# Weight units 64 bytes on in the ring of a hybrid retention and neighbourhood-attention block, with three products split in two

## The chip, the cores and the metric

The kernel runs on one core of one Trainium2 chip. The metric is the device time of one launch in microseconds (us). One matmul instruction of TensorE (PE) multiplies a stationary operand of 128 x 128, the weights of the array, which a separate instruction loads (PEld), by a moving operand of 128 rows and up to 512 columns that is read from on-chip memory (SBUF), and adds the product up in an accumulator bank. VectorE (DVE), ScalarE (ACT) and GpSimd (POOL) do the elementwise work, SyncE (SP) issues most of the transfers.

## The reference

Two layers over 256 latent and 256 context tokens of width 1024. Layer 0 mixes by retention with 4 heads (for both kinds of tokens), layer 1 by neighbourhood attention with 32 heads (latent tokens only, with keys and values from all 512). A squared-relu MLP of 4096 hidden units follows each. Shifts, scales and gates come from a conditioning vector.

```python
for i in range(DEPTH):                      # 2 layers
    mod = silu(c) @ ada_w[i] + ada_b[i]     # shifts, scales, gates; the same for the context
    h = x * (1.0 + sc1) + sh1
    hc = ctx * (1.0 + sc1c) + sh1c
    y, yc = mixer(h, hc)                    # retention in layer 0, neighbourhood attention in layer 1
    x = layer_norm(DN_ALPHA * x + g1 * y, ln_g[i, 0], ln_b[i, 0])
    h = x * (1.0 + sc2) + sh2
    x = layer_norm(DN_ALPHA * x + g2 * sq_relu_mlp(h, mlp_w1[i], mlp_w2[i]), ln_g[i, 1], ln_b[i, 1])
    # layer 0 does the same for ctx
```

## The kernel before

**Products.** All large products are made from float32 numbers split in a high and a low part, both in the fast 32-bit matmul type (fp32r). A product is three passes into one accumulator, high by high, high by low, low by high (`mm3`, line 174). In the program's names `hTh` and `hTl` are the high and low parts of the activations, transposed, 8 blocks of 512 token columns; `hi` and `lo` are those of the weights. The three passes of one block therefore read in the trace `hTh,hi`, `hTl,hi`, `hTh,lo`: first the moving operand, then the weights.

**Stages and moving widths.** Layer 0's projections move 512 columns (`pq`, `pv`, `pg`, `pw`). Its MLP moves 512 columns too, but for the first two of eight pairs of hidden blocks in the first half: there the latent tokens go first (256 columns, `mm1(..., LAT, ...)`), then the context tokens (256 columns, `ctx_mm1`, line 1278), because the context's layer norm is not done yet. In layer 1 the queries and the first pair of key blocks move 256 columns (`pn`; `q_mm`, line 1461, and `k_mm`), the other keys and the values 512 (`pn`, `pnv`). Layer 1's MLP moves 256 columns with an offset: its activations are stored from column `AT = 7 * LINE` on (line 1949), 448 bytes into each block; `p1t` is its first part.

**The weights' ring.** Weights arrive in units of 512 KB, 128 partitions by 1024 numbers (four blocks of 256 columns or two of 512). SP's queue transfers a unit into one of four raw tiles; ACT casts it to the high part; DVE subtracts to get the low part (`fetch`, line 258; `lows`, line 284). High parts go round in a pool `hip` of five tiles and low parts in a pool `lop` of five (lines 139 and 140), and `take` (line 289) has units prepared up to five ahead of their use. The eight chunks of the first stage use the same pools (`Weights.high` and `.low`, lines 763 and 768).

**Where things stand.** Small constants (`lnT`, `cT`, `scol`, `bcol`, `acol`, `misc`, `lgn`, four `mod` tiles) stand in one pool, `cpool`, ahead of `hTh` and of everything large; pools follow each other without gaps. Sizes before, in bytes for each partition: 16384 for each of `hTh` and `hTl`, 4096 for each raw, high or low tile. All of these are multiples of 128, so from a block of `hTh` or `hTl` to any weight block the distance is a multiple of 128 bytes, but in layer 1's MLP, where 448 bytes make it an odd multiple of 64. `LINE` is 16 numbers, 64 bytes. In the built program `hTh` starts at byte 40608 of a partition, which is 32 past a multiple of 64.

**The order of work.** Each engine runs its instructions in order. In the first MLP's early part and in the whole of layer 1's mixer PE, ACT and DVE are held to the program's order (`InOrder` with `on` set). Elsewhere a scheduler puts instructions in the order of their readiness by its own estimate; SP is always held to the program's order.

Of the kernel before, what the change touches and what calls it, by code (L numbers as in the profile page):

```python
# [10 lines left out]
F32 = mybir.dt.float32  # L11
F32R = mybir.dt.float32r
# [5 lines left out]
P = 128  # L18
D = 1024
KC = D // P  # L20
# [4 lines left out]
DK = 256  # L25
DV = 512
# [10 lines left out]
LINE = 16  # L37
# [67 lines left out]
def kernel(  # L105
# [23 lines left out]
    pe, act, dve, pool, sp = (  # L129
        InOrder(tc, getattr(nc, e), e in PIN)  # L130
        for e in ("tensor", "scalar", "vector", "gpsimd", "sync")
    )
    ec = ctx.enter_context

    WB = 5
    smp = ec(tc.tile_pool(name="smp", bufs=4))
    cpool = ec(tc.tile_pool(name="cpool", bufs=1))
    rawp = ec(tc.tile_pool(name="rawp", bufs=4))
    hip = ec(tc.tile_pool(name="hip", bufs=WB))
    lop = ec(tc.tile_pool(name="lop", bufs=WB))  # L140
# [11 lines left out]
    def nm(s):  # L152
        uid[0] += 1
        return f"{s}_{uid[0]}"
# [4 lines left out]
    def slot(i, shape, dt, s):  # L159

        return arena.tile(shape, dt, tag=f"s{i}", name=nm(s))

    def scr(s, dt=F32):
        return scp.tile([P, 512], dt, tag="scr", name=nm(s))

# [5 lines left out]
        act.copy(out=hi_ap, in_=raw_ap)  # L171
        (eng or dve).tensor_sub(out=lo_ap, in0=raw_ap, in1=hi_ap.bitcast(F32))

    def mm3(o, a, b, start, stop):
        (ah, al), (bh, bl) = a, b
        pe.matmul(o, lhsT=ah, rhs=bh, start=start, stop=False)
        pe.matmul(o, lhsT=ah, rhs=bl, start=False, stop=False)
        pe.matmul(o, lhsT=al, rhs=bh, start=False, stop=stop)


# [1 line left out]

    specs = []

    def w_rows(wt, r0, nr, c0, ncol):
        specs.append((wt[r0 : r0 + nr, c0 : c0 + ncol], nr // P, ncol))

    WI, WO = ret_w_in[0], ret_w_o[0]
# [12 lines left out]
            for u in range(2):  # L201
                w_rows(WO, h * DV + u * 256, 256, half * 512, 512)

    def spec_w1(l, f0):
        for u in range(2):
            w_rows(mlp_w1[l], 512 * u, 512, f0, 256)

    for hf in range(2):
        for fp in range(8):
            spec_w1(0, hf * 2048 + fp * 256)  # L210
        for half in range(2):
            for u in range(8):
                w_rows(mlp_w2[0], hf * 2048 + u * 256, 256, half * 512, 512)

    NW, NWO = nat_w_in[0], nat_w_o[0]

    def spec_nq(base, gp):
        for u in range(2):
            w_rows(NW, 512 * u, 512, base + gp * 256, 256)

    def spec_nv(half):
        for u in range(4):
# [31 lines left out]
    units = []  # L254
# [3 lines left out]
    def fetch(n, in_scratch=False, at=None):  # L258

        for src, k, ncol in specs[len(units) : len(units) + max(n, 0)]:  # L260
            raw = rawp.tile([P, k, ncol], F32, tag="raw", name=nm("raw"))
            sp.dma_start(out=raw[:], in_=src.rearrange("(k p) n -> p k n", p=P))
            if len(units) in scaled_units:
                dve.tensor_mul(
                    out=raw[:], in0=raw[:], in1=scale_row[0].unsqueeze(1).broadcast_to([P, k, ncol])
                )
            if in_scratch or len(units) in scratch_units:
                hi, lo = Rows([scr("hi", F32R) for _ in range(k)]), Rows([scr("lo", F32R) for _ in range(k)])
                for i in range(k):
                    act.copy(out=hi[:, i, :], in_=raw[:, i, :])  # L270
                    pending.append((lo[:, i, :], raw[:, i, :], hi[:, i, :]))
                units.append((hi, lo))
                continue
            if at is None:
                hi = hip.tile([P, k, ncol], F32R, tag="hi", name=nm("hi"))
                lo = lop.tile([P, k, ncol], F32R, tag="lo", name=nm("lo"))
            else:
                both = slot(at, [P, 2, k, ncol], F32R, "hilo")
                hi, lo = both[:, 0], both[:, 1]
            act.copy(out=hi[:], in_=raw[:])  # L280
            pending.append((lo[:], raw[:], hi[:]))
            units.append((hi, lo))
# [32 lines left out]

    ident = cv("ident")

    lnT = cpool.tile([P, 2, 2, 2, KC], F32, tag="lnT", name="lnT")
    cT = cpool.tile([P, KC, 16, 2], F32, tag="cT", name="cT")
    scol = cpool.tile([P, 2, KC], F32, tag="scol", name="scol")  # L320
    bcol = cpool.tile([P, 2, KC], F32, tag="bcol", name="bcol")
    acol = cpool.tile([P, 3, 2, KC], F32, tag="acol", name="acol")
    COLUMNS = (0, 1), (1, 0), (1, 1)
    lns = dram.tile([64, P], F32, tag="lns", name="lns")

# [40 lines left out]
    still = scr("still", F32R)  # L366
    dve.memset(still[:, :256].bitcast(F32), 1.0)

    misc = cpool.tile([P, 40], F32, tag="misc", name="misc")
    mhalf, onecol, lgm = misc[:, 0:1], misc[:, 1:34], misc[:, 36:40]  # L370
    dve.memset(mhalf[:], -0.5)

    lgn = cpool.tile([P, 2, 8], F32, tag="lgn", name="lgn")
    mods = {}
    for l in range(2):
        for w in range(2):
            mods[l, w] = cpool.tile([P, 2, KC, 2], F32, tag=f"mod{l}{w}", name=f"mod{l}{w}")

# [219 lines left out]
    def hs(k, a, b):  # L598
        return hTh[:, k, a:b], hTl[:, k, a:b]
# [152 lines left out]
    class Weights:  # L752
# [9 lines left out]

        def high(self, cols=slice(0, DK + DV)):
            if cols.start == 0:
                self.hi = hip.tile([P, DK + DV], F32R, tag="hi", name=nm("hi"))
            act.copy(out=self.hi[:, cols], in_=self.raw[:, cols])

        def low(self, cols=slice(0, DK + DV)):
            if cols.start == 0:
                self.lo = lop.tile([P, DK + DV], F32R, tag="lo", name=nm("lo"))  # L770
# [150 lines left out]
    w = ws[0]  # L921
# [98 lines left out]
    for h in range(RH):  # L1020
# [9 lines left out]
        else:  # L1030
# [148 lines left out]
        if not last:  # L1179
            for half in range(2):  # L1180
                us = take(2)
# [6 lines left out]
        else:  # L1188
# [41 lines left out]
            f0 = affine(0, p0)  # L1230
# [38 lines left out]
    def mm1(us, sl, pb, ks=range(KC), at=0):  # L1269
        for i in range(2):  # L1270
            for k in ks:
                wh, wl = us[k // 4]
                mm3(
                    pb[i][:, sl], (wh[:, k % 4, tsl(i)], wl[:, k % 4, tsl(i)]),
                    hs(k, at + sl.start, at + sl.stop), k == 0, k == KC - 1,
                )

    def ctx_mm1(us, pb):
# [13 lines left out]
    for hf in range(2):  # L1292
# [9 lines left out]
        if hf == 0:  # L1302
            us = take(2, 2, 1)
            pbs = [[bank("p1") for _ in range(2)] for _ in range(2)]
            hts = [hslot(fp) for fp in range(2)]
            mm1(us, LAT, pbs[0], range(0, 4))
            lows(1)
            shift = shift_of(*m3)
            f2 = affine(2, turn(2))
            fetch(1)  # L1310
            low21 = mod_high(f2[1], 1, 2)
            white(3, shift, m3[1])
            low20 = mod_high(f2[0], 0, 2)
# [45 lines left out]
        for half in range(2):  # L1359
            last = hf == 1 and half == 1  # L1360
            pb = [bank("p2") for _ in range(4)]
# [64 lines left out]
            p = turn(0)  # L1426
            mm2(2, 5, held[1])
            f = affine(0, p)
# [7 lines left out]
            p = turn(1)  # L1436
            f = affine(1, p)
# [36 lines left out]

    def q_evac(p):
# [384 lines left out]
    n = NS - 1  # L1860
# [20 lines left out]
    us = take(2, 0)  # L1881
# [53 lines left out]
    mv0, r0 = moments(0)  # L1935
# [300 lines left out]
```

## Time and profile before

| quantity | value |
|---|---|
| median of three runs | 1171.04 us (1170.99, 1171.04, 1173.9) |
| profiled execution's own time | 1175.97 us |
| its span in the trace | 1174.0 us |
| granted clock over the span | 0.995 |
| PE busy | 1163.1 us (99%), 6687 matmul records |
| DVE, ACT, POOL busy | 72%, 41%, 16% |
| PE's share of the chain that ended last | 94% |

In the views of the profile a row of the timeline or of the chain of waits starts with its start in us and its length in us; then come the engine, the line of the code (always 84, the helper through which all instructions go, so one reads by names), the operation, out<-in by the program's names, the shapes, and the number of instructions that were put together. The length of a matmul includes its way through the array, and matmuls overlap: how fast PE goes is read from the distance between starts.

### The profile page before, as it was taken

How to read it: one execution, taken by the hardware profiler on the slowest of the kernel's cores; microseconds unless marked ns; L12 is line 12 of the kernel's file. 1: busy time of each engine (PE TensorE's matmuls, PEld its weight loads, DVE VectorE, ACT ScalarE, POOL GpSimd, SP SyncE). 2: the span in 40 equal slices, each digit the busy share in tenths (PEclk: the TensorE clock that was granted, in tenths of full speed). 3: DMA queues.
4: the chain of work that ended last, by engine and by line, in shares of the span. 5: the costliest groups of instructions: out<-in, count | busy, mean ns of one | idle time of the engine just before them, and what ended most of it. 6: DMA issues, size and time to landing. Idle time of an engine off the chain costs nothing.

```text
span 1174.0 us, 17497 instructions
## 1 busy us (share of the span) xinstructions
PE 1163.1 (99%) x6687; PEld 983.5 (84%) x6687; DVE 846.2 (72%) x1393; ACT 476.6 (41%) x833; POOL 193.3 (16%) x352
## 2 busy tenths in 40 slices
PE   9999999999999999999999999999999999999997
PEld 6788888888888889888888888889878878999886
DVE  3796687788798878678866775568566578877456
ACT  2653321332223246442112333137466566756341
POOL 0102001010220237600311011121222221000001
PEclk8999999999999999999999999999999999999999
DMA  9943453545355426636666666625234235666761
GB/s 274 261 146 108 144 172 116 147 140 176 112 174 160 133 72 222 223 114 215 182 213 192 203 211 189 210 90 180 72 116 125 84 111 160 212 207 204 241 198 54
DMA packets 134164, 192.54 MB, mean 164 GB/s; under 512 B 7265, under 2 KB 77489, under 8 KB 134081
## 3 DMA queue, kind: packets, MB, share of 16 engines
q1 hardware_dynamic: 129888, 178.36, 48.5%
q0 software_dynamic: 3136, 10.63, 2.9%
q10 hardware_dynamic: 1056, 2.44, 0.7%
q8 instruction: 52, 0.85, 0.3%
q14 instruction: 32, 0.25, 0.1%
HBM read 185.06 MB, written 6.35 MB: 163 GB/s over the span
## 4 chain that ended last, share of the span: by engine, by line
PE 94%; DVE 2%; ACT 1%; DMA 1%; issue 1%; POOL 0%; ACTq 0%; DVEq 0%; SPq 0%
PE p L84 44%; PE pq L84 8%; PE pv L84 8%; PE pw L84 7%; PE pg L84 7%; PE pn L84 5%; PE pnv L84 4%; PE po L84 2%; PE pnw L84 2%; PE ppt L84 1%; PE pS L84 1%; PE pav L84 1%; PE pt L84 1%; PE pada L84 1%; PE pqk L84 1%; PE p1t L84 1%
## 5 line engine op out<-in xcount | busy, mean ns | idle before, releaser
L84 ACT CAST hi<-raw 128x1024 fp32r<-128x1024 f32 (+2 forms) x228 | 231.9, 1033 | 298.8 <-PE p L84 130.8
L84 DVE TENSOR_TENSOR lo<-raw,hi 128x1024 fp32r<-128x1024 f32 (+2 forms) x228 | 272.7, 1212 | 91.2 <-ACT hi L84 91.0
L84 PE MATMUL p<-hi,hid 128*128 128x512 f32 (+1 forms) x780 | 237.9, 386 | 0.0
L84 PEld LDWEIGHTS p<-hi,hid 128*128 128x128 f32 x780 | 145.7, 188 | 29.4
L84 PE MATMUL p<-hTl,hi 128*128 128x256 f32 (+1 forms) x512 | 165.9, 326 | 0.0
L84 PE MATMUL p<-hTh,lo 128*128 128x256 f32 (+1 forms) x512 | 165.9, 326 | 0.0
L84 PE MATMUL p<-hTh,hi 128*128 128x256 f32 (+1 forms) x512 | 162.6, 327 | 0.0
L84 PE MATMUL p<-lo,hid 128*128 128x512 f32 (+1 forms) x390 | 150.5, 386 | 0.0
L84 DVE SCALAR_TENSOR_TENSOR acc<-rawa,scol,acc 128x1024 f32<-128x1024 f32 x56 | 73.4, 1318 | 63.8 <-DMA rawa<-in_ada_w_dram 63.5
L84 PEld LDWEIGHTS p<-hTl,hi 128*128 128x128 f32 x512 | 96.4, 188 | 8.7
L84 PEld LDWEIGHTS p<-hTh,lo 128*128 128x128 f32 x512 | 96.3, 188 | 8.7
L84 PEld LDWEIGHTS p<-hTh,hi 128*128 128x128 f32 x512 | 94.3, 188 | 8.8
L84 PEld LDWEIGHTS p<-lo,hid 128*128 128x128 f32 x390 | 73.3, 188 | 14.7
L84 DVE SCALAR_TENSOR_TENSOR strips<-rawa,scol,strips 128x512 f32<-128x512 f32 x112 | 78.5, 762 | 0.0
L84 ACT CAST hid<-r 128x256 fp32r<-128x256 f32 (+1 forms) x64 | 31.9, 500 | 108.4 <-DVE r L84 108.3
L84 POOL TENSOR_TENSOR rstd<-rstd,misc 128x1 f32<-128x1 f32 x28 | 19.1, 684 | 222.1 <-DVE rstd L84 221.1
L84 PE MATMUL pw<-hi,oh 128*128 128x512 f32 x128 | 50.7, 396 | 0.0
L84 PE MATMUL pg<-hi,hTh 128*128 128x512 f32 x128 | 50.6, 395 | 0.0
L84 PE MATMUL pw<-hi,ol 128*128 128x512 f32 x128 | 50.0, 391 | 0.1
L84 PE MATMUL pg<-hi,hTl 128*128 128x512 f32 x128 | 49.9, 390 | 0.0
L84 PE MATMUL pq<-hTh,hi 128*128 128x512 f32 x128 | 49.7, 399 | 0.1
L84 PE MATMUL pg<-lo,hTh 128*128 128x512 f32 x128 | 49.8, 389 | 0.0
(241 smaller groups left out, 2227.6 us busy)
## 6 DMA issues: line engine op xcount, KB each, us to landing
raw<-in_mlp_w_dram SPq DMA_DIRECT2D x128, 512.0 KB, 4.5
rawa<-in_ada_w_dram SPq DMA_DIRECT2D x80, 512.0 KB, 3.8
raw<-in_ret_w_in_dram SPq DMA_DIRECT2D x42, 512.0 KB, 4.0
raw<-in_nat_w_in_dram SPq DMA_DIRECT2D x24, 512.0 KB, 4.3
rawq<-in_ada_w_dram SPq DMA_DIRECT2D x16, 512.0 KB, 6.0
raw<-in_ret_w_o_dram SPq DMA_DIRECT2D x16, 512.0 KB, 3.5
bias<-rpb_all POOLq DMA_DIRECT2D x16, 256.0 KB, 3.5
raw<-in_nat_w_o_dram SPq DMA_DIRECT2D x8, 512.0 KB, 3.5
```

Of the source, the lines that this page charges most:

```text
L84: r = f(*args, **kwargs)
```

## The change

The two pools of the ring become five, `w0` to `w4`, each with one tile that holds a high part and its low part behind one another (`wpair`). A tile has room for 2 x 1024 numbers and 16 more (64 bytes; 128 more, 512 bytes, in the last two). `w_rows` notes for each unit a `place`, 0 or `LINE`: at `LINE` both parts start 64 bytes on in their tile. Noted so are the units of layer 0's first two pairs of hidden blocks, all units of the queries, and the first pair of the keys. Between the first three of the five pools stand pools of 448 bytes with the small constants; from the start of one ring tile to the next it is 8192 + 64 + 448 = 8704 bytes, a multiple of 128. `cT` goes to a slot of the arena that is used again later, `misc` grows from 40 to 48 numbers. `cpool` is thereby 2336 bytes shorter, and everything large stands that much lower: `hTh` starts at byte 38272, a multiple of 64 and of 128. `mm3` can split its middle pass in two of 128 columns each, and does so in three products: at k = 5 of block 0 in the two `mm1` calls that start with k = 4, and at k = 5 of block 0 of the first pair of queries.

```diff
-    hip = ec(tc.tile_pool(name="hip", bufs=WB))
-    lop = ec(tc.tile_pool(name="lop", bufs=WB))
+    wps, gaps = [], []
+    for i in range(WB):
+        wps.append(ec(tc.tile_pool(name=f"w{i}", bufs=1)))
+        if i < 3:
+            gaps.append(ec(tc.tile_pool(name=f"gap{i}", bufs=1)))
...
+    WSLOT = 1024
+    visits = [0]
+
+    def wpair(at=0):
+
+        i = visits[0] % WB
+        visits[0] += 1
+        both = wps[i].tile([P, 2 * WSLOT + (LINE if i < 3 else P)], F32R, tag="w", name=nm("w"))
+        return both[:, at : at + WSLOT], both[:, at + WSLOT : at + 2 * WSLOT]
...
-    def mm3(o, a, b, start, stop):
+    def mm3(o, a, b, start, stop, parted=False):
         (ah, al), (bh, bl) = a, b
         pe.matmul(o, lhsT=ah, rhs=bh, start=start, stop=False)
-        pe.matmul(o, lhsT=ah, rhs=bl, start=False, stop=False)
+        if parted:
+            for c in (slice(0, P), slice(P, 2 * P)):
+                pe.matmul(o[:, c], lhsT=ah, rhs=bl[:, c], start=False, stop=False)
+        else:
+            pe.matmul(o, lhsT=ah, rhs=bl, start=False, stop=False)
         pe.matmul(o, lhsT=al, rhs=bh, start=False, stop=stop)
...
-            spec_w1(0, hf * 2048 + fp * 256)
+            spec_w1(0, hf * 2048 + fp * 256, LINE if hf == 0 and fp < 2 else 0)
...
-            w_rows(NW, 512 * u, 512, base + gp * 256, 256)
+            w_rows(NW, 512 * u, 512, base + gp * 256, 256, LINE if base == 0 or gp == 0 else 0)
...
-                hi = hip.tile([P, k, ncol], F32R, tag="hi", name=nm("hi"))
-                lo = lop.tile([P, k, ncol], F32R, tag="lo", name=nm("lo"))
+                hi, lo = (w.rearrange("p (k n) -> p k n", k=k) for w in wpair(places[len(units)]))
...
-    lnT = cpool.tile([P, 2, 2, 2, KC], F32, tag="lnT", name="lnT")
-    cT = cpool.tile([P, KC, 16, 2], F32, tag="cT", name="cT")
+    lnT = gaps[0].tile([P, 2, 2, 2, KC], F32, tag="lnT", name="lnT")
+    cT = arena.tile([P, KC, 16, 2], F32, tag="s1", name="cT")
...
-    misc = cpool.tile([P, 40], F32, tag="misc", name="misc")
+    misc = gaps[2].tile([P, 3 * LINE], F32, tag="misc", name="misc")
...
-            mm1(us, LAT, pbs[0], range(4, KC))
+            mm1(us, LAT, pbs[0], range(4, KC), parted=5)
...
-            mm1(us[2:4], LAT, pbs[1], range(4, KC))
+            mm1(us[2:4], LAT, pbs[1], range(4, KC), parted=5)
...
-                    k == 0, k == KC - 1,
+                    k == 0, k == KC - 1, (p, i, k) == (0, 0, 5),
```

The order of PE's instructions differs at the three splits alone; POOL's and SP's don't differ. This is PE at the first of the splits, layer 0's MLP, behind the transposes (`pt`) of a context tile; `p_621` before and `p_552` after are the same accumulator. Before:

```order
L84 MATMUL pt_3875<-cst_81,xn_3594 128x128 x4
L84 MATMUL p_621_3837<-hTh,hi_3785 128x256
L84 MATMUL p_621_3837<-hTl,hi_3785 128x256
L84 MATMUL p_621_3837<-hTh,lo_3786 128x256
L84 MATMUL p_621_3837<-hTh,hi_3785 128x256
L84 MATMUL p_621_3837<-hTl,hi_3785 128x256
L84 MATMUL p_621_3837<-hTh,lo_3786 128x256
```

And after, where `w` is the tile with both parts, so that the third pass of a product and the first of the next read alike and stand as x2:

```order
L84 MATMUL pt_3824<-cst_99,xn_3545 128x128 x4
L84 MATMUL p_552_3786<-hTh,w_3736 128x256
L84 MATMUL p_552_3786<-hTl,w_3736 128x256
L84 MATMUL p_552_3786<-hTh,w_3736 128x256 x2
L84 MATMUL p_552_3786<-hTl,w_3736 128x128 x2
L84 MATMUL p_552_3786<-hTh,w_3736 128x256 x2
L84 MATMUL p_552_3786<-hTl,w_3736 128x256
```

The fifth pass behind the transposes is two of 128 columns now; the rest stands as before.

Where the order is the scheduler's, ACT and DVE change at some 70 places each, all of one kind. This is ACT in layer 0's MLP: casts of units (`hi` before, `w` after) and evacuations of hidden blocks (`ACTIVATE r`, `CAST hid`). Before:

```order
L84 ACTIVATE r_4299<-p_653_4225 128x512
L84 CAST hid_4224<-r_4299 128x512
L84 CAST hi_4316<-raw_4314 128x1024
L84 CAST hi_4322<-raw_4320 128x1024
L84 ACTIVATE r_4304<-p_654_4226 128x512
L84 CAST hid_4224<-r_4304 128x512
```

And after:

```order
L84 ACTIVATE r_4244<-p_582_4174 128x512
L84 CAST hid_4173<-r_4244 128x512
L84 CAST w_4261<-raw_4259 128x1024
L84 ACTIVATE r_4249<-p_583_4175 128x512
L84 CAST w_4266<-raw_4264 128x1024
L84 CAST hid_4173<-r_4249 128x512
```

The cast of a pair's second unit stands behind one evacuation where it stood ahead of it: with both parts in one tile, the tile comes free with the last read of its low part, one matmul later than its high part did.

More of the change, by code (lines that the diff above doesn't have):

```diff
@@ L172, in split, with w_rows @@
         (eng or dve).tensor_sub(out=lo_ap, in0=raw_ap, in1=hi_ap.bitcast(F32))
-    def mm3(o, a, b, start, stop):
+    def mm3(o, a, b, start, stop, parted=False):
         (ah, al), (bh, bl) = a, b
         pe.matmul(o, lhsT=ah, rhs=bh, start=start, stop=False)
-        pe.matmul(o, lhsT=ah, rhs=bl, start=False, stop=False)
+        if parted:
[3 more added lines that the diff above has]
+            pe.matmul(o, lhsT=ah, rhs=bl, start=False, stop=False)
         pe.matmul(o, lhsT=al, rhs=bh, start=False, stop=stop)
     specs = []
-    def w_rows(wt, r0, nr, c0, ncol):
+    places = {}
+    def w_rows(wt, r0, nr, c0, ncol, place=0):
+        places[len(specs)] = place
         specs.append((wt[r0 : r0 + nr, c0 : c0 + ncol], nr // P, ncol))
@@ L202, with spec_w1 @@
                 w_rows(WO, h * DV + u * 256, 256, half * 512, 512)
-    def spec_w1(l, f0):
+    def spec_w1(l, f0, place=0):
         for u in range(2):
-            w_rows(mlp_w1[l], 512 * u, 512, f0, 256)
+            w_rows(mlp_w1[l], 512 * u, 512, f0, 256, place)
     for hf in range(2):
         for fp in range(8):
-            spec_w1(0, hf * 2048 + fp * 256)
+            spec_w1(0, hf * 2048 + fp * 256, LINE if hf == 0 and fp < 2 else 0)
         for half in range(2):
@@ L316 @@
     ident = cv("ident")
-    lnT = cpool.tile([P, 2, 2, 2, KC], F32, tag="lnT", name="lnT")
-    cT = cpool.tile([P, KC, 16, 2], F32, tag="cT", name="cT")
-    scol = cpool.tile([P, 2, KC], F32, tag="scol", name="scol")
-    bcol = cpool.tile([P, 2, KC], F32, tag="bcol", name="bcol")
-    acol = cpool.tile([P, 3, 2, KC], F32, tag="acol", name="acol")
+    lnT = gaps[0].tile([P, 2, 2, 2, KC], F32, tag="lnT", name="lnT")
+    cT = arena.tile([P, KC, 16, 2], F32, tag="s1", name="cT")
+    scol = gaps[1].tile([P, 2, KC], F32, tag="scol", name="scol")
+    bcol = gaps[2].tile([P, 2, KC], F32, tag="bcol", name="bcol")
+    acol = gaps[0].tile([P, 3, 2, KC], F32, tag="acol", name="acol")
     COLUMNS = (0, 1), (1, 0), (1, 1)
@@ L367 @@
     dve.memset(still[:, :256].bitcast(F32), 1.0)
-    misc = cpool.tile([P, 40], F32, tag="misc", name="misc")
+    misc = gaps[2].tile([P, 3 * LINE], F32, tag="misc", name="misc")
     mhalf, onecol, lgm = misc[:, 0:1], misc[:, 1:34], misc[:, 36:40]
     dve.memset(mhalf[:], -0.5)
-    lgn = cpool.tile([P, 2, 8], F32, tag="lgn", name="lgn")
+    lgn = gaps[2].tile([P, 2, 8], F32, tag="lgn", name="lgn")
     mods = {}
@@ L376 @@
         for w in range(2):
-            mods[l, w] = cpool.tile([P, 2, KC, 2], F32, tag=f"mod{l}{w}", name=f"mod{l}{w}")
+            mods[l, w] = gaps[1 + l * w].tile([P, 2, KC, 2], F32, tag=f"mod{l}{w}", name=f"mod{l}{w}")
     RR = [cpool.tile([P, 2, D], F32, tag=f"R{t}", name=f"R{t}") for t in range(2)]
@@ L764, in high @@
             if cols.start == 0:
-                self.hi = hip.tile([P, DK + DV], F32R, tag="hi", name=nm("hi"))
+                self.hi, self.lo = (w[:, : DK + DV] for w in wpair())
             act.copy(out=self.hi[:, cols], in_=self.raw[:, cols])
         def low(self, cols=slice(0, DK + DV)):
-            if cols.start == 0:
-                self.lo = lop.tile([P, DK + DV], F32R, tag="lo", name=nm("lo"))
             dve.tensor_sub(out=self.lo[:, cols], in0=self.raw[:, cols], in1=self.hi[:, cols].bitcast(F32))
@@ L1267, with mm1 @@
     LAT, ALL, CTX = slice(0, NLAT), slice(0, NT), slice(NLAT, NT)
-    def mm1(us, sl, pb, ks=range(KC), at=0):
+    def mm1(us, sl, pb, ks=range(KC), at=0, parted=None):
         for i in range(2):
@@ L1274, in mm1 @@
                     pb[i][:, sl], (wh[:, k % 4, tsl(i)], wl[:, k % 4, tsl(i)]),
-                    hs(k, at + sl.start, at + sl.stop), k == 0, k == KC - 1,
+                    hs(k, at + sl.start, at + sl.stop), k == 0, k == KC - 1, (i, k) == (0, parted),
                 )
```

## The prediction

> **What bounds the kernel now.** I read the page's head first, then the chain of waits, then the timeline of PE.
>
> ```profile
> span 1174.0 us, 17497 instructions
> PE 1163.1 (99%) x6687; PEld 983.5 (84%) x6687; DVE 846.2 (72%) x1393; ACT 476.6 (41%) x833; POOL 193.3 (16%) x352
> PE 94%; DVE 2%; ACT 1%; DMA 1%; issue 1%; POOL 0%; ACTq 0%; DVEq 0%; SPq 0%
> ```
>
> TensorE is busy throughout and makes 94% of the chain that ended last: the time is the number of matmuls times the distance between their starts, and waits elsewhere are short. So the change can act where those distances change, and only where no other wait takes the gain. The chain shows the stretches in question (start, length, number of matmuls):
>
> ```profile
> 439.60 2.87 PE p L84 x24
> 443.34 5.75 PE p L84 x48
> 449.96 331.30 PE p L84 x1518
> 792.57 2.87 PE pn L84 x24
> 796.38 5.76 PE pn L84 x48
> 803.01 3.11 PE pn L84 x26
> 806.13 11.53 PE pn L84 x94
> 881.94 5.94 PE pn L84 x48
> 927.74 11.47 PE pn L84 x72
> ```
>
> 5.75 us for 48 is 120 ns a matmul. The timeline gives it finer. The first two rows lie 90 matmuls apart, the next two 40, the next two 100, the last two 44 (of 512 columns):
>
> ```profile
> 451.94 0.28 PE L84 MATMUL p<-hTh,hi 128*128 128x256 f32 x1
> 462.75 0.28 PE L84 MATMUL p<-hTh,lo 128*128 128x256 f32 x1
> ...
> 1003.00 0.28 PE L84 MATMUL p<-hTh,hi 128*128 128x256 f32 x1
> 1007.71 0.28 PE L84 MATMUL p<-hTl,hi 128*128 128x256 f32 x1
> ...
> 1010.00 0.28 PE L84 MATMUL p<-hTh,lo 128*128 128x256 f32 x1
> 1021.34 0.28 PE L84 MATMUL p<-hTh,hi 128*128 128x256 f32 x1
> ...
> 599.99 0.39 PE L84 MATMUL p<-hi,hid 128*128 128x512 f32 x1
> 609.96 0.39 PE L84 MATMUL p<-lo,hid 128*128 128x512 f32 x1
> ```
>
> So the same shape with the same operands goes at 120.1 ns in layer 0's MLP (10.81/90), and at 117.8 (4.71/40) or 113.4 (11.34/100) in layer 1's. In the code only the place differs: there the 256 columns start 448 bytes into their block, so the moving operand stands an odd multiple of 64 bytes from the weights that are loaded meanwhile; in layer 0 the distance is a multiple of 128. I call this half-off. It has two rates, and what precedes a stretch sets which:
>
> ```profile
> 994.34 8.03 PE p1t L84 x68
> 1002.81 5.66 PE p L84 x48
> 1008.90 158.03 PE p L84 x1026
> ...
> 1002.21 0.60 PE L84 MATMUL pt<-cst,r 128*128 128x128 f32 x4
> 1008.30 0.60 PE L84 MATMUL pt<-cst,r 128*128 128x128 f32 x4
> ```
>
> The 68 and the 48 (8.03/68 = 118 ns) keep the middle rate to their end, the stretch from 1008.9 runs at the quick one; both of the last two begin behind four transposes (the two lower rows), so transposes leave either rate. Once set, it holds.
>
> **The change part by part.** *The places.* After the change 480 matmuls of 256 columns stand half-off: the stretches of 24 (439.6), 48 (443.3), 120 (at the head of the row at 449.96), 24, 48, 26 and 94 (792 to 817.6), 48 (881.9) and 48 (first part of the row at 927.7). At the quick rate each saves 120.0 - 113.3 = 6.7 ns, at the middle one 2.2. If nothing else waited that would be 480 x 6.7 = 3.2 us or 1.1.
>
> *The splits.* Two parts of 128 columns in place of one pass cost an interval more. A 128-column interval is bounded below by the transposes' row (1.42/13 = 109 ns) and above by half the 256-column one plus nothing, which would make the split free:
>
> ```profile
> 830.52 1.42 PE ppt L84 x13
> ```
>
> I take 109 ns for each part, as that is the only measured 128-column interval, so a split costs 2 x 109 - 113 = 0.11 us; free at best. In the order it stands fifth behind transposes in the stretches of 443.3, 449.96 and 796.4. There it can do one thing: a disturbance that puts the stream on the quick rate, as something did at 1008.9. No row shows that a split does it. Without it those stretches are as likely middle as quick.
>
> *Sum over stretches.* At 439.6 the stretch comes straight from 512-column matmuls, where even before the first distance is 113 to 120 ns; 24 x 6.7 = 0.16, less a start, 0.15 us. At 443.3: 48 x 6.7 = 0.32, less the split 0.11 and 0.04 for four matmuls ahead of it, 0.17; at the middle rate 48 x 2.2 - 0.11 = 0. At 449.96: 120 x 6.7 = 0.80 - 0.11 - 0.05 = 0.64, or 0.15. Nothing waits in the 331.3 us of that row, so these stay on the path.
>
> The next three (24, 48, 26) end in a wait:
>
> ```profile
> 805.84 0.28 PE L84 MATMUL pn<-hTl,hi 128*128 128x256 f32 x1
> 806.13 0.38 PE L84 MATMUL pn<-hTh,lo 128*128 128x256 f32 x1
> 806.13 0.19 PEld L84 LDWEIGHTS pn<-hTh,lo 128*128 128x128 f32 x1 [0.21 <-DVE lo L84]
> 804.86 2.35 DVE L84 TENSOR_TENSOR lo<-raw,hi 128x1024 fp32r<-128x1024 f32 x2
> ```
>
> DVE makes the low parts back to back with other work that began before 794 and doesn't depend on these matmuls' pace; if PE comes 0.3 us sooner it waits 0.3 us longer. Nothing is gained, and the third split is free. The 94 behind that wait are on the path again: 94 x 6.7 = 0.63, 0.60 with its start; 0.19 at the middle rate. I expect quick there, since a wait precedes it.
>
> The 48 at 881.9 run into ACT and DVE work that has no pause from 883 on, and PE waits for its end:
>
> ```profile
> 887.46 2.39 DVE L84 TENSOR_TENSOR lo<-raw,hi 128x1024 fp32r<-128x1024 f32 x2 [2.09 <-ACT hi L84]
> 899.68 1.14 DVE L84 COPY pt<-ppt 128x384 f32<-128x384 f32 x2
> ```
>
> Gain 0. The 48 at 927.7 have DVE waiting for their result, so they count:
>
> ```profile
> 939.64 0.42 DVE L84 TENSOR_TENSOR kT<-pn,kT 128x256 fp32r<-128x256 f32 x1 [0.90 <-ACT kT L84]
> ```
>
> They give 48 x 6.7 = 0.32, 0.28 with the start, or 0.09. The sum is 0.15 + 0.17 + 0.64 + 0.60 + 0.28 = 1.84 us all quick, 0.15 + 0 + 0.15 + 0.19 + 0.09 = 0.58 with every stretch behind the first at the middle rate. I take 1.45, some two thirds of the way, as three of the four uncertain starts have a wait or a split just behind them, like the quick ones in the trace.
>
> *One tile for both parts.* The cast of a second unit comes behind one evacuation, and tiles come free one matmul later (0.12 to 0.23 us). In layer 0's MLP, from 464 to 785 us, ACT and DVE have this to do (number, busy us and mean ns, idle ahead and its releaser):
>
> ```profile
> L84 ACT CAST hi<-raw 128x1024 fp32r<-128x1024 f32 x58 | 60.1, 1052 | 119.3 <-PE p L84 92.2 <-DMA raw<-in_mlp_w_dram 26.8
> L84 DVE TENSOR_TENSOR lo<-raw,hi 128x1024 fp32r<-128x1024 f32 x58 | 70.8, 1232 | 13.1 <-ACT hi L84 13.1
> L84 ACT ACTIVATE r<-p 128x512 f32<-128x512 f32 x28 | 16.6, 592 | 18.0 <-PE p L84 18.0
> ```
>
> The cover is the lead of the ring: a unit in use covers 24 matmuls, 24 x 0.2267 = 5.4 us, and cast and subtraction take 1.05 + 1.23 = 2.3 us with units up to five ahead. An evacuation of 0.59 us and one matmul more are hidden there. In the mixer of layer 1, where the lead is shorter, the cost is at most one matmul late at each of two places where a cast waits for PE, 0.23 us; I take 0. The transfers are the same and SP's order too; `cT` in the arena is written and read before that slot's next use, at no cost.
>
> Subtracted from the profiled execution, the span goes from 1174.0 to about 1172.5. The median of the runs was 1171.04 where the profiled one took 1175.97; part of that is the clock of its first microseconds:
>
> ```profile
> 12.80:17.40 4.60, 4.58 (x14) 3.18 (x17) 1.95 (x4) 1.37 (x3) 0.00 (x0) 0.50 1.17 309
> 14.86 1.71 PE pv L84 x4
> 22.12 0.93 PE pv L84 x4
> ```
>
> The granted clock is 0.50 there, and the same four matmuls take 1.71 us in place of 0.93; over the some ten microseconds at that clock I estimate 2 to 3 us, which is about the distance of 1173.9 from 1171.0 in the three runs. So a median after can land 2.9 us high by this alone. The Trainium skill ("TensorE: Matmul & The Clock Gate", "Part 1: The HAM clock gate (the "warmup" mystery)") has half rate until a free-running window has seen the engine busy; the row agrees.
>
> **The rivals.** *All at the middle rate:* neither split nor wait moves the stream, as at 1002.8, and 0.58 us are left: 1170.5. For it speaks that two of three stretches behind short interruptions in layer 1 were at 117.8.
>
> *The place makes no difference here:* layer 1's pace has another reason, and only two splits count, +0.22 us: 1171.3. Against it: the operands and shapes are the same at 120.1 and 113.4. The Trainium skill (the same page, "Step-by-step: what each phase is for") says that the weights and the moving operand have independent read ports, and that loading the next weights takes no read bandwidth from the running matmul; by that this rival would be right. The trace's 120.1 against 113.4 doesn't fit it.
>
> *The small shift speeds everything:* all large tiles now stand on a multiple of 64 bytes where they stood 32 past one. If the 226.6 ns of a 512-column matmul (9.97/44) hold something for reads that straddle, 3942 such matmuls save 3.9 us for each ns. From 0.6 ns on the kernel is faster by more than 0.3%; 2 ns would give 1161.7. For it: 256 columns at 113.4 are 0.443 ns a column and transposes, whose identity stands at a multiple of 64, have the lowest interval, 109. Against it: no row has the same shape at both places, and 226.6 is 2 x 113.3, with nothing left over for an edge.
>
> *The small shift slows everything,* the rival on the other side: the same 3942 matmuls, if multiples of 64 for both operands collide where 32 past did not, as multiples of 128 between them cost 256-column ones 6.7 ns. From 0.4 ns a matmul (1.6 us) it eats the gain, from 1.3 ns it is slower by 0.3%; 2 ns would give 1169.6 + 7.9 = 1177.5. Against it: distances between tiles modulo 128 stay as they were for all 512-column products, and 120 against 113 went by distance.
>
> **How the numbers follow.** The forecast has 55%: 1171.04 - 1.45 = 1169.6, with a range of its own of 1169.0 to 1170.6. The middle rate has 16%, no difference 6%, the speed-up by the shift 15%, the slowdown 8%. What a measurement of this kernel tells from no change is about 0.3%, 3.5 us: faster is below 1167.5, slower above 1174.6. The first three cases all lie inside; so same 0.77, faster 0.15 by the fourth, slower 0.08 by the fifth. The range reaches from 1167.6, the start of the fourth case, to 1172.8, the forecast with the late clock and half of the smallest slowdown.
>
> **What would show it.** Starts 113 to 114 ns apart in the stretches at 439, 443, 450, 806 and 928, and 118 where a start stayed middle; behind each split the rate changes or it doesn't. The wait that ended at 806.13 grows by 0.3 to 0.5 us, and so does the one behind the 48 at 882. Distances of 512-column matmuls stay 226.7; any other number there means the fourth or fifth case, and the forecast is wrong by 3.9 us for each ns. ACT's casts behind an evacuation must not appear as releasers of PE between 464 and 785 us.

## The result: 0.24% slower

The changed kernel takes 1174.86 us in the median of 22 runs (1173.07 to 1176.68), the kernel before 1171.69 in 22 runs beside it (1170.94 to 1175.88). The ratio is 1.0024, with a 95% interval of 1.0018 to 1.003: some 3 us slower, inside the 0.3% that the prediction called no change, but outside its range of 1167.6 to 1172.8 and on the other side of its forecast of 1169.6.

The profile of the changed kernel has a span of 1172.8 us, 1.2 us less than the one before. This must not be read as a gain: the execution profiled before had the late clock of its first microseconds, and this one has it not.

```profile
span 1172.8 us, 17502 instructions
PE 1160.5 (99%) x6690; PEld 980.6 (84%) x6690; DVE 846.4 (72%) x1393; ACT 478.6 (41%) x833; POOL 191.3 (16%) x352
PE 92%; DVE 3%; ACT 2%; DMA 1%; issue 1%; POOL 0%; DVEq 0%; SPq 0%; ACTq 0%; POOLq 0%
PEclk9999999999999999999999999999999999999999
```

TensorE's part of the chain that ended last fell from 94% to 92%: PE, busy to the same share, now waits somewhere where it did not. To find the place, each matmul's start after is compared with the start of the same matmul before, both from their span's start (worked out from the two traces; a number that grows is time lost):

```
time in the trace of before (us)   30     430     465     785     806     824     861     864    1160
start after less start before    -4.52   -4.48   -5.28   -5.28   -5.29   -1.60   -1.60   -1.17   -1.12
```

The first 4.5 us are the late clock. Then 0.80 us are won between 430 and 465, where 0.96 were forecast; nothing up to 806, as forecast; and at 806 to 824 3.7 us are lost, on balance: 0.6 us are won there too, by the 94 matmuls near 806. Another 0.43 go at 861 to 864. From 430 us to the end the change costs 3.36 us in these two executions; the medians of the runs lie 3.17 us apart.

**The gain is there.** These are rows of the chain of waits after, to hold against the rows at 439.60, 443.34 and 449.96 before:

```profile
435.12 2.83 PE p L84 x24
438.82 5.62 PE p L84 x49
445.32 330.66 PE p L84 x1519
```

The second and third have one matmul more, the split. 2.87, 5.75 and 331.30 became 2.83, 5.62 and 330.66: 0.04, 0.13 and 0.64 us won, where the prediction had 0.15, 0.17 and 0.64. Everything of 512 columns in the 330.66 us goes as before, at 226.7 ns: standing on a multiple of 64 bytes, where they stood 32 past one, makes no difference for the large tiles.

**The loss** is a wait of ACT. First ACT in the timeline before, then after:

```profile
809.83 2.00 ACT L84 CAST hi<-raw 128x1024 fp32r<-128x1024 f32 x2
811.73 0.45 ACT L84 ACTIVATE qT<-pn 128x128 fp32r<-128x128 f32 x2
```

```profile
804.55 1.05 ACT L84 CAST w<-raw 128x1024 fp32r<-128x1024 f32 x1
810.46 1.05 ACT L84 CAST w<-raw 128x1024 fp32r<-128x1024 f32 x1 [4.85 <-PE pn L84]
811.42 0.77 ACT L84 ACTIVATE qT<-pn 128x128 fp32r<-128x128 f32 x4
811.88 1.14 DVE L84 SCALAR_TENSOR_TENSOR qT<-pn,qT 128x64 fp32r<-128x64 f32 x8 [5.02 <-ACT qT L84]
812.99 0.40 ACT L84 CAST kT<-pn 128x256 fp32r<-128x256 f32 x1
813.45 0.46 PE L84 MATMUL pqk<-kT,qT 32*128 32x416 f32 x4 [1.66 <-ACT kT L84]
814.55 0.65 PE L84 MATMUL pqk<-kT,qT 32*128 32x416 f32 x8 [0.64 <-DVE kT L84]
```

Before, ACT casts two units in one go; after, the second of these casts waits 4.85 us for PE. Order is held to the program's here, so the evacuation of the queries (`qT`) and of the keys (`kT`) queue up behind the cast on ACT, DVE waits 5.02 us for ACT, and the scores (`pqk`) make PE wait 1.66 and 0.64 us. What the cast waits for is shown by the ring's tiles (address in the partition, first and last start of a matmul that reads it, worked out from the trace and the built program):

```
                      before (high part)             after (both parts)
keys, unit 1          114336   799.10 to 815.82      113024   793.87 to 810.15
keys, unit 2          106144   800.54 to 817.26      121728   795.28 to 811.51
queries, unit 1       102048   805.72 to 808.62      130432   800.40 to 803.35
queries, unit 2        97952   808.86 to 811.50       95616   803.46 to 806.07
values, unit 1        110240   from 818.35           104320   from 815.13
values, unit 2        102048   from 819.85           113024   from 817.57
```

The keys' units are held for 16 us, since two groups of heads read them with other work between; the queries' that were taken after them come free first. One pool of five tiles gave the second unit of values the tile of the queries, free at 808.62. Five pools of one tile, asked in a fixed turn, give it that of the keys, free at 810.15, though another has been free since 803.35.

The pause costs once more by the clock. The windows' columns are PE, PEld, DVE, ACT and POOL busy, granted clock, DMA share and rate:

```profile
810.00:814.00 4.00, 2.24 (x20) 1.78 (x18) 2.12 (x9) 3.54 (x8) 0.00 (x0) 1.00 0.35 133
814.00:815.10 1.10, 0.55 (x8) 0.30 (x8) 1.10 (x3) 1.10 (x3) 0.00 (x0) 1.00 0.00 0
815.10:818.60 3.50, 3.50 (x13) 2.76 (x10) 3.50 (x10) 2.71 (x5) 0.00 (x0) 0.56 0.82 208
...
815.20 7.29 PE pnv L84 x24
```

After 2.3 us of idle PE within 5.1 us the granted clock is 0.56 on average over the next 3.5 us, and the 24 matmuls of the chain's row take 7.29 us where the same 24 took 5.67 before at the full clock (first the chain's row there, then the window):

```profile
818.42 5.67 PE pnv L84 x24
818.40:821.60 3.20, 3.20 (x18) 2.66 (x15) 3.20 (x9) 3.17 (x7) 0.00 (x0) 1.00 0.65 193
```

So this place costs 4.3 us (3.7 on balance and the 0.6 won by the 94): 2.7 us up to the end of the scores, of which 2.3 are idle, and 1.6 us of half clock, against 1.4 us won there and ahead of it.

### The profile page after: what moved, and what is told of

It reads as the page before. It is cut to its first block, busy times and chain, and to the rows that moved or that the text cites. A ratio compares the mean times of both kernels' runs of the same rounds, so it can differ in the third digit from the quotient of the medians.

```text
span 1172.8 us, 17502 instructions
## 1 busy us (share of the span) xinstructions
PE 1160.5 (99%) x6690; PEld 980.6 (84%) x6690; DVE 846.4 (72%) x1393; ACT 478.6 (41%) x833; POOL 191.3 (16%) x352
## 4 chain that ended last, share of the span: by engine, by line
PE 92%; DVE 3%; ACT 2%; DMA 1%; issue 1%; POOL 0%; DVEq 0%; SPq 0%; ACTq 0%; POOLq 0%
PE p L84 43%; PE pq L84 8%; PE pv L84 8%; PE pw L84 7%; PE pg L84 7%; PE pnv L84 4%; PE pn L84 3%; PE po L84 2%; PE pnw L84 2%; PE ppt L84 1%; PE pS L84 1%; PE pav L84 1%; PE pada L84 1%; ACT w L84 1%; PE pt L84 1%
## 5 line engine op out<-in xcount | busy, mean ns | idle before, releaser
L84 ACT CAST w<-raw 128x1024 fp32r<-128x1024 f32 (+2 forms) x224 | 231.7, 1040 | 320.7 <-PE p L84 155.2
L84 DVE TENSOR_TENSOR w<-raw,w 128x1024 fp32r<-128x1024 f32 (+2 forms) x224 | 271.8, 1221 | 97.1 <-ACT w L84 96.8
L84 PE MATMUL p<-w,hid 128*128 128x512 f32 (+1 forms) x1158 | 260.0, 386 | 0.0
L84 PEld LDWEIGHTS p<-w,hid 128*128 128x128 f32 x1158 | 214.9, 188 | 43.6
L84 PE MATMUL p<-hTh,w 128*128 128x256 f32 (+1 forms) x1024 | 237.8, 326 | 0.0
L84 PEld LDWEIGHTS p<-hTh,w 128*128 128x128 f32 x1024 | 171.2, 188 | 17.4
L84 PE MATMUL p<-hTl,w 128*128 128x256 f32 (+2 forms) x514 | 165.4, 325 | 0.0
L84 PEld LDWEIGHTS p<-hTl,w 128*128 128x128 f32 x514 | 96.4, 188 | 8.8
L84 PE MATMUL pq<-hTh,w 128*128 128x512 f32 x256 | 80.1, 392 | 0.4 <-DVE hTh L84 0.4
L84 PE MATMUL pw<-w,oh 128*128 128x512 f32 x256 | 79.9, 393 | 0.0
```

The source lines that it names most:

```text
L84: r = f(*args, **kwargs)
```

## Experiments

Three theories stood at the start. *Fixed turn:* the loss is the order in which tiles are handed out. *Shared tile:* it is that both parts of a unit come free together. *Place:* it is the 64 bytes. The first four kernels ran side by side (before: 1172.58 us).

**One pool in place of five.** The changed kernel with a pool of five tiles; the constants go back to `cpool`.

```diff
-    for i in range(WB):
-        wps.append(ec(tc.tile_pool(name=f"w{i}", bufs=1)))
...
+    wp = ec(tc.tile_pool(name="wp", bufs=WB))
+    gaps = [cpool] * 3
...
-        i = visits[0] % WB
-        visits[0] += 1
-        both = wps[i].tile([P, 2 * WSLOT + (LINE if i < 3 else P)], F32R, tag="w", name=nm("w"))
+        both = wp.tile([P, 2 * WSLOT + 2 * LINE], F32R, tag="w", name=nm("w"))
```

> The changed kernel with one pool of five ring tiles in place of five pools of one tile each (the small constants go back ahead of the large tiles; places, splits and the shared tile for both parts stay). Theory 'fixed turn': the loss came from the tiles being handed out in a fixed turn, so that the cast of the second unit of values waited 4.85 us for the tile of the first keys; with a free choice that wait and the half clock behind it go, and the 1.3 us gained before it stay: 1.1 to 1.4 us faster than before. Rival 'shared tile': the loss came from both parts coming free together; then as slow as the changed kernel, 3 us slower than before. Rival 'place': the 64 bytes themselves cost; also 3 us slower.

Measured: 1182.11 us, ratio 1.008 (1.0065 to 1.0096), slower than every theory had it. The stall near 812 us was gone, and yet time was lost all along the way:

```profile
449.41 336.11 PE p L84 x1519
```

The long stretch takes 336.11 us, 5.4 more than in the changed kernel. I had made tiles of 8320 bytes, 65 x 128, to save room, so that from one tile to the next the distance changes by 128 modulo 256; the changed kernel has 8704, 34 x 256, and the kernel before 4096. Grouped by the distance from the moving operand to the next weights, the 512-column matmuls of this trace average 228.3 ns between starts where it is a multiple of 256 (2073 of them) and 232.8 where it is 128 off (1734); all are at multiples of 256 before, and average 227.2. The rule that I had looked at, multiples of 128, was too coarse. (For all but some 80 of these matmuls the distance to their own weights is the same modulo 256, so that it is the next weights that count isn't shown.)

**The fixed turn alone.** The kernel before, its two pools of five made ten pools of one; no splits, no places, parts apart, addresses as before.

```diff
-    hip = ec(tc.tile_pool(name="hip", bufs=WB))
-    lop = ec(tc.tile_pool(name="lop", bufs=WB))
+    hips = [ec(tc.tile_pool(name=f"hip{i}", bufs=1)) for i in range(WB)]
+    lops = [ec(tc.tile_pool(name=f"lop{i}", bufs=1)) for i in range(WB)]
...
+        i = wturn[which] % WB
...
-                hi = hip.tile([P, k, ncol], F32R, tag="hi", name=nm("hi"))
-                lo = lop.tile([P, k, ncol], F32R, tag="lo", name=nm("lo"))
+                hi = wring("hi", [P, k, ncol])
+                lo = wring("lo", [P, k, ncol])
...
```

> The kernel before with its two pools of five made ten pools of one, handed out in a fixed turn; addresses, places and order of the program as before, no splits, parts in tiles of their own. Theory 'fixed turn': the whole loss without the gain, 4.2 to 4.6 us slower than before (some 2.6 us of stall near 812 us of the trace and 1.6 us of half clock behind it). Rivals 'shared tile' and 'place': no difference.

Measured: 1175.64 us, ratio 1.0029 (1.0016 to 1.0043), 3.1 us slower by the medians where 4.2 to 4.6 were expected; the interval reaches from 1.9 to 5.0 us. In its trace, against that of before, 4.0 us are lost between 806 and 824 us, and the rows are those of the changed kernel:

```profile
811.43 1.05 ACT L84 CAST hi<-raw 128x1024 fp32r<-128x1024 f32 x1 [5.26 <-PE pn L84]
814.42 0.47 PE L84 MATMUL pqk<-kT,qT 32*128 32x416 f32 x4 [1.47 <-ACT kT L84]
815.10:818.60 3.50, 3.08 (x13) 2.21 (x14) 3.50 (x8) 2.71 (x4) 0.00 (x0) 0.56 0.55 168
...
1008.12 160.82 PE p L84 x1026
```

The fixed turn makes the loss without the shared tile and without the places. The two rivals, which had no difference here, aren't needed for it; whether they add to it is read from the kernel with tiles of 8448 bytes below. The last row is a thing by itself: the long stretch of layer 1's MLP, 158.03 us before, took 160.82 in this execution. Its 624 matmuls of 256 columns were at 117.8 ns in place of 113.3.

**No places.** The kernel of the one pool with every unit at place 0.

```diff
-            spec_w1(0, hf * 2048 + fp * 256, LINE if hf == 0 and fp < 2 else 0)
+            spec_w1(0, hf * 2048 + fp * 256, 0)
...
-            w_rows(NW, 512 * u, 512, base + gp * 256, 256, LINE if base == 0 or gp == 0 else 0)
+            w_rows(NW, 512 * u, 512, base + gp * 256, 256, 0)
```

> The kernel of the one pool with all units at place 0; splits stay. If the 64 bytes make the gain: 120 ns again in all nine stretches, 0.2 us slower than before by two splits on the path. If the lower addresses of everything (a multiple of 64 where 32 past one) made part of the gain: faster than before by that part.

Measured: 1183.46 us, to be held against 1182.11 with places in the same tiles: the places are worth 1.35 us by the medians of five and six runs. In its trace the nine stretches end at 118.5 to 120.0 ns again. (Against before the time can't be read, because of the 8320 bytes.)

**Every unit placed.** The kernel of the one pool, all of the ring's units 64 bytes on but layer 1's first MLP weights.

```diff
-    def w_rows(wt, r0, nr, c0, ncol, place=0):
+    def w_rows(wt, r0, nr, c0, ncol, place=LINE):
...
-            w_rows(mlp_w1[l], 512 * u, 512, f0, 256, place)
+            w_rows(mlp_w1[l], 512 * u, 512, f0, 256, place if l else LINE)
...
-            w_rows(NW, 512 * u, 512, base + gp * 256, 256, LINE if base == 0 or gp == 0 else 0)
+            w_rows(NW, 512 * u, 512, base + gp * 256, 256, LINE)
```

> The kernel of the one pool with every unit of the ring 64 bytes on but layer 1's first MLP weights (which are half-off by their columns already); 3571 matmuls of 512 columns stand half-off. If a 512-column matmul loses time to its neighbour's weights as a 256-column one does (6.7 ns each): 220 ns between starts and up to 24 us faster. If 226.7 ns is its own pace and hides the weights: the same as the one pool with few units placed, within 0.5 us.

Measured: 1185.83 us, ratio 1.0107 (1.0093 to 1.0122); the long stretch went from 336.11 to 337.74 us:

```profile
451.56 337.74 PE p L84 x1519
```

Half-off is no gain for 512 columns, but a loss: 229.5 ns where the distance is 64 modulo 256, 233.1 where it is 192. Neither expectation was right; for this width multiples of 256 are best.

**One pool, tiles of 8448 bytes.** The first experiment again, 33 x 256 in place of 65 x 128.

```diff
-        both = wp.tile([P, 2 * WSLOT + 2 * LINE], F32R, tag="w", name=nm("w"))
+        both = wp.tile([P, 2 * WSLOT + 4 * LINE], F32R, tag="w", name=nm("w"))
```

> The one pool again with tiles of 8448 bytes (33 x 256) in place of 8320 (65 x 128); nothing else differs from the first kernel of the one pool. There 512-column matmuls whose operand stood 128 bytes off (modulo 256) from the next weights took 232.8 ns between starts, the others 228.3, and before 226.7. Theory 'modulo 256, and fixed turn': all 512-column distances are multiples of 256 again, 226.7 ns, no stall near 812 us: 1.1 to 1.4 us faster than before. Rival 'one pool': something else of the one pool costs 10 us; then again 1182. Rival 'shared tile': a stall of 3 to 4 us near 812 us as in the changed kernel, 1175.

Measured: 1170.63 us beside 1171.48, ratio 0.9992 (0.9983 to 1.0001), 11.5 us less than with 8320 bytes; 0.85 us faster than before where 1.1 to 1.4 were expected, with an interval that reaches to no gain at all. The long stretch is at 330.67 us, the pause and the half clock are gone:

```profile
446.00 330.67 PE p L84 x1519
805.23 2.00 ACT L84 CAST w<-raw 128x1024 fp32r<-128x1024 f32 x2
812.39 0.84 PE L84 MATMUL pqk<-kT,qT 32*128 32x416 f32 x12
813.22 5.64 PE pnv L84 x24
815.10:818.60 3.50, 3.50 (x17) 2.80 (x15) 3.50 (x8) 2.65 (x9) 1.80 (x3) 1.00 0.64 184
```

Both casts go in one again, with the shared tile in place. So the shared tile and the places cost nothing that shows there, and the fixed turn was the loss. Of the 1.4 us won by 824, 0.5 were given back at 861 to 864 in this profile, as in the one of the changed kernel: there the scores wait for work that waited for a late transfer of the bias table (two rows of this kernel, then one of the changed kernel):

```profile
857.23 0.90 PE L84 MATMUL pqk<-kT,qT 32*128 32x416 f32 x10 [0.35 <-ACT pt L84]
849.45 0.59 DVE L84 CUSTOM_DVE_ANT_0 s<-pqk,bias 128x416 f32<-128x416 f32 x1 [0.41 <-DMA bias<-rpb_all]
...
853.02 0.59 DVE L84 CUSTOM_DVE_ANT_0 s<-pqk,bias 128x416 f32<-128x416 f32 x1 [0.36 <-DMA bias<-rpb_all]
```

In the three profiles of the next experiment, where PE came just as early, it did not happen; in that of the last one it did. What sets it stays open.

**Without splits, and with one.** The same kernel without the three splits, measured twice, and with the split at the head of the long stretch alone. The diff leads from none to that one.

```diff
-            mm1(us[2:4], LAT, pbs[1], range(4, KC))
+            mm1(us[2:4], LAT, pbs[1], range(4, KC), parted=5)
```

> The same without the three splits. If a split moves the stream from 117.8 to 113.3 ns: the stretches of 48 and 120 near 443 and 450 us stay at 117.8, 168 x 4.5 = 0.76 us lost and 0.23 us of two splits saved, 0.5 us slower than with splits. If the quick rate came by itself there: 0.2 us faster than with splits.

> The one pool of 8448-byte tiles without splits, again and beside the kernel with one split. If the split sets the rate near 450 us: 117.8 ns there again, 0.4 us slower than its neighbour. If the rate is chance: 113.3 ns there this time or the next.

> The one pool of 8448-byte tiles with the split at the head of the long stretch (near 450 us) alone. If a split moves the stream there: the 120 matmuls at 113.3 ns in place of the 117.8 they had without any split, 0.54 less 0.11, 0.4 us faster than without splits, and 0.1 us faster than with three: 0.9993 or less of the kernel before. If splits are chance: 117.8 ns there.

Measured: without splits 1170.51 us beside 1170.63 with three, 0.1 us faster where the split's effect was to make it 0.5 us slower; then 1170.74, and with the one split 1170.28 beside it, 0.46 us faster, as expected. The first pair hides the effect: by the traces the kernel with three splits is 0.39 us ahead from 430 to 861 us, and gives that back at the late transfer. Rows of the chain of waits, the two without splits first, the one with a split last:

```profile
445.88 331.05 PE p L84 x1518
801.78 10.95 PE pn L84 x94
```

```profile
445.18 331.05 PE p L84 x1518
801.09 11.35 PE pn L84 x94
```

```profile
439.06 5.62 PE p L84 x48
445.55 330.67 PE p L84 x1519
801.08 10.94 PE pn L84 x94
```

The long stretch's 120 matmuls were at 117.8 ns twice without a split, and at 113.3 in all five profiles with a split and units 64 bytes on (the changed kernel, three splits at 8320 and at 8448 bytes, every unit placed, one split). So the split sets the rate there. In the stretch of 48 near 439 us, the rate was quick without it too; it takes 5.62 us all the same, since one distance of 224 ns in its middle loses there what the split costs. At the third place, near 791 us, the stream stayed at 117.8 ns after the split in the changed kernel and with 8448 bytes. The 94 near 801 us (10.95 us in the first profile, 11.35 in the second, 10.94 in the third) were at 117.8 and at 113.3 ns in two kernels that don't differ there, and also at 113.3 in the first profile, whose kernel is that of the second: chance. This chance is worth 0.4 us in an execution, so that the 0.46 us between the medians can't all be put down to the split; the long stretch's rows show 0.38.

The kernel with one split is the fastest of the study. Its ratio to the kernel before is 0.9969 (0.9957 to 0.9981), which flatters it: 14 of the 23 runs of before beside it took 1173.9 us or more, the other nine 1170.9 to 1171.5. Held against those nine it is 1.1 us faster.

**192 bytes on.** The kernel of 8448 bytes with three splits, the placed units 192 bytes on in place of 64.

```diff
-            spec_w1(0, hf * 2048 + fp * 256, LINE if hf == 0 and fp < 2 else 0)
+            spec_w1(0, hf * 2048 + fp * 256, 3 * LINE if hf == 0 and fp < 2 else 0)
...
-            w_rows(NW, 512 * u, 512, base + gp * 256, 256, LINE if base == 0 or gp == 0 else 0)
+            w_rows(NW, 512 * u, 512, base + gp * 256, 256, 3 * LINE if base == 0 or gp == 0 else 0)
```

> The one pool of 8448-byte tiles with the placed units 192 bytes on in place of 64, so that the distance from the moving operand to the weights is 64 modulo 256, not 192. If only the odd multiple of 64 counts: the same as with 64 within 0.3 us, 113.3 or 117.8 ns in the nine stretches. If the place within 256 bytes counts for 256 columns as it does for 512 (229.5 against 233 ns): a distance between starts other than 113.3 in the long stretch at 450 us, 120 x 1 ns = 0.1 us for each ns.

Measured: 1171.36 us, ratio 1.0002 (0.9993 to 1.0011), 0.7 us slower than with 64 bytes. All nine stretches ran at 117.8 ns to their end, those with a split and those behind a wait as well:

```profile
445.61 331.14 PE p L84 x1519
801.61 11.34 PE pn L84 x94
```

The late transfer of the bias table is in this profile too and takes 0.63 us at 861 to 864 (0.49 with 64 bytes); ahead of it, from 430 us on, this kernel falls 1.1 us behind the one with 64 bytes by the two traces. So not every odd multiple of 64 does. The quick rate was reached in layer 0's MLP and in the mixer where the distance from the moving operand to the weights is 192 modulo 256, and in this kernel, where it is 64, nowhere there. A row of the prediction fits this: the 68 matmuls of `p1t` at 994.34 have the weights' units as moving operands, so their distance is 64, and they went at 117.8 ns in every profile with tiles at multiples of 256. But the distance alone is not the whole of it: in the first kernel of one pool the 48 matmuls near 443 us stand at 64 as well and reached 113.3 ns, and with every unit placed they stand there too and went at 117.8. What decides stays open.

## Why the prediction was wrong

*The sum of the gain* was right in its size. 1.45 us were forecast; the kernel with one split, which has none of the loss, gains 1.39 us from 430 us to the end by its trace. By terms: 0.04, 0.13 and 0.64 at the first three stretches against 0.15, 0.17 and 0.64 (the first was at the middle rate, which a start straight from 512-column matmuls was thought to rule out); 0.59 at the 94 against 0.60 (11.53 before, 10.94 with one split). That the total comes so near is in part luck: 1.84 was cut to 1.45 for starts that might be at the middle rate, and what was missing was 0.28 at the last stretch and 0.11 at the first, while the quick rate at the 94 was chance.

*The stretches that end in waits* went as said ahead of 806 and 900 us: nothing gained there. Ahead of 900 the wait did take 0.29 us; ahead of 806 there was little to take, as the three stretches went at 117.8 ns and the split cost its part. The last one, 48 near 928, was put at 0.28 and brought 0: PE came 0.30 us sooner to 934 us and lost it by 950. A row of the changed kernel that has no like before shows where, at the unit that follows the 48:

```profile
935.47 0.30 PEld L84 LDWEIGHTS pn<-hTh,w 128*128 128x128 f32 x2 [0.44 <-DVE w L84]
```

The idle time of DVE quoted in the prediction showed that DVE waits for these matmuls a little later; that PE would first wait for DVE's low part was overlooked.

*The splits* cost what was said, 0.11 us, and one of three does something: it sets the rate in the long stretch. (The prediction's two bounds for a distance of 128 columns stand the wrong way round: half of a 256-column one, 57 ns, is below 109.)

*The failed step* is "One tile for both parts". It counted how much later a tile comes free, one matmul, and put the cost in layer 1's mixer at 0 with 0.23 us at most. It did not ask which tile is handed out. The lines of the diff said it, `wps[i]` with `i = visits[0] % WB`: a pool of five may give the one that is free, five pools of one may not. That is worth 4.3 us in the changed kernel, 2.7 up to the end of the scores and 1.6 of clock; the fixed turn alone, in a kernel without any other part of the change, loses 4.0 us at the same place. The rival on the other side was about addresses, and no rival was about the ring. The wait to be foreseen was in the trace of before: units of keys that are read from 799 to 817 us, while the queries' units taken after them were done at 808.6 and 811.5.

*The two cases of the small shift* fell: 512-column distances did not change. But their mechanism, an address that costs 512-column matmuls some ns each, exists at 128 bytes modulo 256, and the gaps of constants between the ring's places, which make 8704 of 8256 bytes, keep the change clear of it. The prediction had seen multiples of 128 alone.

*The late clock* was sized wrongly. It was put at 2 to 3 us and held to be the distance from 1171.0 to 1173.9. By the first 20 us of the traces it costs 4.3 to 4.6 us, which is about the distance to the runs at 1175.9. (The range's upper end, 1172.8, doesn't follow from its terms either: 1169.6 with 2.9 and half of 1.6 is 1173.3. The measured 1174.86 lies above both.) Nor does the row at 12.80 show by itself that the rate rises once a window has seen the engine busy: PE was busy for 4.58 of its 4.60 us, and the clock was at half all the while. The 2.8 us fit another thing, layer 1's long stretch at 117.8 in place of 113.3 ns: 624 x 4.5 ns = 2.8, as one execution of the fixed turn shows. That the runs of before at 1174 are these is an inference; none was profiled.

## What to carry to other kernels

When a ring of tiles is taken apart, into pools of one or tiles by index, list for each unit its last reader and check that the tile whose turn it is comes free no later than the one that a free choice would take; units that live longer than their successors are where it breaks. A pause of 2.3 us on a busy TensorE cost 1.6 us more by the clock here. And where weights are cast into a ring beside their moving operands, keep the distances between tiles at multiples of 256 bytes for 512-column products before trying anything finer.

## What the runs showed of the hardware

- The distance between starts of fp32r matmuls depends on the place of the moving operand against the weights, modulo 256 bytes (grouped here by the next weights; the matmul's own nearly always stand at the same distance). With 512 columns: 226.7 ns at 0 (228.3 in a trace with other distances mixed in), 232.8 at 128, 229.5 at 64, 233.1 at 192. With 256 columns: 120.0 at 0; 113.3 or 117.8 at 192; 117.8 alone at 64 with the units 192 bytes on, though the kernel with 8320-byte tiles, where the units stand at 64 and 192 by turns, reached 113.3 at both. The Trainium skill ("TensorE: Matmul & The Clock Gate", "Step-by-step: what each phase is for") has two independent read ports and no loss by loading the next weights; that the pace depends on the distance at all doesn't fit this, though no run shows that it is the loading that takes the time.
- Of the two rates at 192 the stream keeps the one that its first matmuls set, where all units of a stretch stand at one distance. A middle pass split in two of 128 columns set the quick one at one place in all five profiles that have it with units 64 bytes on; at another it did not in the changed kernel and with 8448 bytes. Behind a wait near 806 us it was chance.
- The granted clock fell to half after 2.3 us of idle time within 5.1 us. The Trainium skill (the same page, "Part 1: The HAM clock gate (the "warmup" mystery)") has it fall after at least one idle window of about 3.4 us; here less was enough.
